# Column halves and quarters of the array in the attention and convolution stage of a two-layer encoder

## The chip, the core and the metric

The kernel runs on one NeuronCore of a Trainium2 chip. The metric is the device time of one launch in microseconds (us). The engines are named as the profile names them: PE is TensorE's matmul, PEld its weight load, DVE is VectorE, ACT is ScalarE, POOL is GpSimd, SP is SyncE, which here only issues DMAs.

## The reference

Two layers, each a half-weighted SwiGLU, a mixing block with attention beside a convolution, a second half-weighted SwiGLU and a norm. There is one sequence of 512 tokens with 1024 features, in float32. What matters here is the mixing block:

```python
def chunk_causal_attention(q, k, v):            # 8 heads, 96 query/key and 64 value features
    for i in range(s // Q_BLOCK):               # query blocks of 128, chunks of 64
        scores = einsum('bhqd,bhkd->bhqk', q[block i], k[: end of block i]) * scale
        scores = where(k_chunk <= q_chunk, scores, -1e30)
        outs.append(einsum('bhqk,bhkd->bqhd', softmax(scores), v))

def conv_group(u_raw, conv_w, conv_b, ln_g, ln_b):
    u = a * sigmoid(g)                          # 512 channels
    y = causal depthwise conv of u, 31 taps; y = y + conv_b
    return silu(layer_norm(y, ln_g, ln_b))

x = x + concatenate([attn, conv]) @ w_out
```

In each block of 128 queries the first 64 must not see the last 64 keys.

## The kernel before

Activations lie with features on the 128 partitions and the 512 tokens along the free axis, so a tile is 128 by 512. Products with big weights are made of three products of operands that are split into a high and a low part (`mm3`, lines 154 to 156). The feed-forward blocks (L373, L374 and most of L154 to L156) take most of the time and are left as they are.

`mix_body` first projects the normed input, then attends, convolves, and projects out. A scheduler of the framework puts the instructions of each engine in order; the order of the source is its priority, and `tc.issue_after` holds a step back until another has been issued. The attention is written as stages of one head each, with lags between them (`ORDER`): `turn` transposes queries and keys (L811, L816, copied by ACT L813 and DVE L818), `scores` makes one product of each block of 128 queries with the keys up to the block's end (L834), adds -1e30 to 64 rows by a small bf16 product (L835), takes the row maximum (DVE L836) and the exponential (ACT L840); `turn_p` transposes the probabilities (L855, copied at L858 by DVE, ACT, DVE); `values` multiplies them with the values (L868), the probabilities as 128 weight columns and the 64 value columns of the head as the moving operand, ten products for a head, and divides by the sums (DVE L875); `turn_out` transposes the result of two heads (L886) and splits it (L161, L162). The attention's operands are plain float32.

The convolution's 512 channels are four groups of 128. `CONV = "DAAD"` says how each is made: groups 0 and 3 on DVE, one instruction for a tap (L922), accumulating in PSUM; groups 1 and 2 with the tap's product on ACT (L926, tile `pr`) and its sum on POOL (L930, tile `y`). Of group 2 thus 30 taps go through ACT and POOL. Then POOL adds the four groups (L944 to L946), PE makes the mean (L948), and while DVE, ACT and POOL finish the LayerNorm, `early_groups` lets PE make the attention's half of three output tiles (`WOG = 3`; `E1`, `E2`, `E3` say at which points). PSUM has seven banks `ps` and one `cv`. Weights come by DMAs that SP issues in order (L136); the low parts of four tiles of `w_out` come by accumulating DMAs from POOL (L142).

Of the kernel before, what the change touches and what calls it, by code (L numbers as in the profile page):

```python
# [7 lines left out]
FP = mybir.dt.float32  # L8
# [3 lines left out]
AF = mybir.ActivationFunctionType  # L12
# [47 lines left out]
JOINED = ("b21", "t3", "t4")  # L60

VECS = [("g1", 8), ("gm", 8), ("g2", 8), ("gp", 8), ("gql", 3), ("gkl", 2),
        ("cw", 4 * CK), ("cb", 4), ("lg", 4), ("lb", 4), ("gq", 1), ("gk", 1)]
VOFF = {}
_o = 0
for _n, _w in VECS:
# [1 line left out]
    _o += _w  # L68
VN = _o
CCOS, CSIN, CID = 0, 64, 128  # L70
CN = 256


@with_exitstack
def encoder_kernel(ctx: ExitStack, tc: tile.TileContext, xT, consts, vecs, rgain, wgu1, wd1, wdq1,
# [11 lines left out]
    def nm(s):  # L87
        uid[0] += 1
        return f"{s}{uid[0]}"
# [7 lines left out]
    def bank():  # L97
        return psum.tile([P, S], FP, tag="ps", name=nm("ps"))
# [517 lines left out]

    def mix_body(kpool, l, gx, norm, done):
        u, order = [], {}

        def kept(dt=FP):  # L620
            return kpool.tile([P, S], dt, tag="m", name=nm("m"), bufs=2 * WIDE)
        ys = [None if kind == "D" else kpool.tile([P, S], FP, tag="y", name=nm("y"), bufs=2) for kind in CONV]

        def glu(pa, pg):
            tg = tmp()
            V.tensor_tensor(tg, pg, R, ALU.mult)
            sg = tmp()
            order["gate"] = A.activation(sg, tg, AF.Sigmoid).ins
            ta = tmp()
            V.tensor_tensor(ta, pa, R, ALU.mult)  # L630
            uc = kept()
            (G if GLUP else V).tensor_tensor(uc, ta, sg, ALU.mult)
# [188 lines left out]
        def scores(h):  # L821
            qT, kT = heads[h]["qk"]
            b01, b2, b3 = bank(), bank(), bank()
            if h % 2 == 0:
                heads[h]["sums"] = small.tile([P, NT, 2], FP, tag="sums", name=nm("sums"), bufs=3)
            sums = heads[h - h % 2]["sums"]
            mx = small.tile([P, NT], FP, tag="mx", name=nm("mx"), bufs=3)
            pi = []
            ps = [slot() for _ in range(3)]
            ps = [ps[0][:, 0:128], ps[0][:, 128:384], ps[1][:, 0:384], ps[2]]  # L830
            for i in range(NT):
                n = (i + 1) * P
                o = (b01[:, 0:128], b01[:, 128:384], b2[:, 0:384], b3)[i]
                T.matmul(o, qT[0:DQ, i * P:(i + 1) * P], kT[0:DQ, 0:n], start=True, stop=False)  # L834
                heads[h]["s"] = T.matmul(o[:, n - 64:n], mrow, mneg, start=False, stop=True).ins  # L835
# [4 lines left out]
                A.activation(p, o, AF.Exp, bias=mx[:, i:i + 1], scale=scqs[i][:, h:h + 1] if QFOLD else 1.0,  # L840
                             accum_out=sums[:, i, h % 2:h % 2 + 1])
                pi.append(p)
            heads[h]["p"] = pi
# [17 lines left out]
        def values(h):  # L861

            if h % 2 == 0:
                heads[h]["po"] = bank()
            po = heads[h - h % 2]["po"].rearrange("p (t h d) -> p t h d", t=NT, h=2)
            for t in range(NT):
                for j in range(t + 1):
                    T.matmul(po[:, t, h % 2], heads[h]["pt"][j][:, (t - j) * P:(t - j + 1) * P],  # L868
                             vs[j][:, h * DV:(h + 1) * DV], start=j == 0, stop=j == t)
            if h % 2 == 0:  # L870
# [4 lines left out]
            V.tensor_tensor(o.rearrange("p (t h d) -> p t h d", t=NT, h=2), po,  # L875
                            rs[:, :, :, None].to_broadcast([P, NT, 2, DV]), ALU.mult)
            heads[h]["o"] = o

        def turn_out(h):

            if h % 2 == 0:
                return
            o = heads[h]["o"]
            ps = bank()
            for t in range(NT):
                T.transpose(ps[:, t * P:(t + 1) * P], o[:, t * P:(t + 1) * P], ident)  # L886
# [27 lines left out]
        for c in range(4):  # L914
            kind = CONV[c]
            acc = psum.tile([P, S], FP, tag="cv", name=nm("cv"), bufs=1) if kind == "D" else ys[c]
            tap = lambda k: cw[:, c * CK + k:c * CK + k + 1]
            A.activation(acc, u[c], AF.Identity, scale=tap(CK - 1), bias=cb[:, c:c + 1])  # L918
            for k in range(CK - 2, -1, -1):
                s = CK - 1 - k  # L920
                if kind == "D":
                    V.scalar_tensor_tensor(acc[:, s:], u[c][:, :S - s], tap(k), acc[:, s:], ALU.mult, ALU.add)  # L922
                    continue
                pr = kpool.tile([P, S], FP, tag="pr", name=nm("pr"), bufs=3)
                if kind == "A":
                    A.activation(pr[:, s:], u[c][:, :S - s], AF.Copy, scale=tap(k))  # L926
                else:
                    G.tensor_scalar(pr[:, s:], u[c][:, :S - s], tap(k), None, ALU.mult)
                with tc.issue_after(order["keys"]) if s >= PAUSE or c > 1 else nullcontext():
                    order["conv"] = G.tensor_tensor(acc[:, s:], acc[:, s:], pr[:, s:], ALU.add).ins  # L930
            if kind == "D":
                A.copy(u[c], acc)
                ys[c] = u[c]
        early = []

        def early_groups(ms):
# [6 lines left out]
        ysum = tmp()  # L943
        G.tensor_tensor(ysum, ys[0], ys[1], ALU.add)  # L944
        G.tensor_tensor(ysum, ysum, ys[2], ALU.add)
        (G if YP else V).tensor_tensor(ysum, ysum, ys[3], ALU.add)  # L946
        pm = bank()
        T.matmul(pm, onesm, ysum, start=True, stop=True)  # L948
        if PRELOAD:
# [291 lines left out]
```

## Time and profile before

| | |
|---|---|
| median of 3 runs | 1800.13 us (1799.9 to 1801.16) |
| the profiled execution | 1798.87 us, span 1797.1 us, granted clock 1.0 |
| PE busy | 1781.8 us, 99% of the span |
| DVE, ACT, POOL busy | 1494.5, 1107.5, 421.5 us |

The span is from the first to the last instruction. The mixing block stands in it twice, with its attention from about 450 to 508 us in layer 0 and from about 1339 to 1398 us in layer 1. A matmul's recorded duration contains its way through the array; what a stream of them costs is read from start to start. A float32 product has two rows in the trace where the program has one.

### The profile page before, as it was taken

The page shows a single profiled execution, that of the slowest core. Times are in us where ns is not written, and L with a number is a line of the kernel's source. Part 1 is how long each engine was busy: PE and PEld are TensorE (multiplying, and loading weights), DVE is VectorE, ACT ScalarE, POOL GpSimd, SP SyncE. Part 2 cuts the span into 40 slices and gives each one's busy share as a digit, 9 for nine tenths or more (in the row PEclk, how much of TensorE's full clock was granted, in tenths as well). Part 3 has the DMA queues.
Part 4 walks back from the last instruction along what each step waited for, and adds up shares of the span by engine and source line. Part 5 has one row for each costly group of instructions (what it writes and reads, how often), then busy time and mean ns, then how long its engine had stood idle before and what let it go on. Part 6 is the DMA issues. An engine that isn't in the chain of part 4 may idle for free.

```text
span 1797.1 us, 29235 instructions
## 1 busy us (share of the span) xinstructions
PE 1781.8 (99%) x11334; PEld 1602.4 (89%) x11334; DVE 1494.5 (83%) x2299; ACT 1107.5 (62%) x1721; POOL 421.5 (23%) x343
## 2 busy tenths in 40 slices
PE   9999999999999999999999999999999999999998
PEld 7899999888788899999888999998978788999997
DVE  7898988589956989898779989876998668989883
ACT  5575756457953575756645757554779435756564
POOL 1000000258943000000310000002689410000002
PEclk9999999999999999999999999999999999999999
DMA  5657575325103466665426575743250125575742
GB/s 168 171 131 182 135 177 123 109 88 134 33 22 102 123 164 161 155 160 132 123 65 170 122 194 122 193 112 111 81 147 7 46 82 160 140 183 134 182 117 74
DMA packets 70413, 226.16 MB, mean 126 GB/s; under 512 B 7937, under 2 KB 8321, under 8 KB 70273
## 3 DMA queue, kind: packets, MB, share of 16 engines
q1 hardware_dynamic: 54000, 169.74, 30.3%
q0 software_dynamic: 16128, 54.53, 18.0%
q8 instruction: 89, 1.46, 0.3%
q14 instruction: 52, 0.42, 0.1%
q10 hardware_dynamic: 144, 0.00, 0.0%
HBM read 222.15 MB, written 2.10 MB: 125 GB/s over the span
## 4 chain that ended last, share of the span: by engine, by line
PE 91%; ACT 3%; DVE 2%; POOL 2%; issue 1%; DMA 0%; SPq 0%; ACTq 0%; POOLq 0%; DVEq 0%
PE ps L154 24%; PE ps L156 23%; PE ps L155 23%; PE ps L373 11%; PE ps L374 6%; PE ps L868 1%; PE ps L834 1%; POOL y L930 1%; ACT pr L926 1%; ACT r L840 1%; PE ps L855 1%; PE ps L198 0%; POOL sck L173 0%; PE ps L217 0%; DVE wl L246 0%
## 5 line engine op out<-in xcount | busy, mean ns | idle before, releaser
L155 PE MATMUL ps<-r,wh 128*128 128x256 f32 (+1 forms) x2540 | 806.8, 318 | 0.0
L154 PE MATMUL ps<-r,wh 128*128 128x256 f32 (+1 forms) x2540 | 803.6, 320 | 2.2 <-ACT wh L138 0.7
L156 PE MATMUL ps<-r,wl 128*128 128x256 f32 (+1 forms) x2348 | 749.2, 321 | 0.0
L154 PEld LDWEIGHTS ps<-r,wh 128*128 128x128 f32 x2540 | 480.5, 189 | 47.0 <-ACT wh L138 3.6
L155 PEld LDWEIGHTS ps<-r,wh 128*128 128x128 f32 x2540 | 481.6, 190 | 35.8 <-DVE r L162 1.5
L156 PEld LDWEIGHTS ps<-r,wl 128*128 128x128 f32 x2348 | 445.1, 190 | 33.5 <-DVE wl L144 0.4
L373 PE MATMUL ps<-xj,wh 128*128 128x512 f32 x864 | 303.9, 392 | 0.0
L138 ACT CAST wh<-raw 128x1024 fp32r<-128x1024 f32 (+3 forms) x148 | 131.9, 899 | 208.1 <-PE ps L155 125.8
L390 POOL DMA_DIRECT2D ls<-in_wgu x72 | 62.7, 871 | 734.7 <-ACT ls L389 595.3
L244 ACT CAST wh<-fr 128x1024 fp32r<-128x1024 f32 (+1 forms) x160 | 157.6, 985 | 104.4 <-DVE fr L410 53.2
L144 DVE TENSOR_TENSOR wl<-raw,wh 128x1024 fp32r<-128x1024 f32 (+3 forms) x132 | 145.3, 1108 | 91.3 <-ACT wh L138 90.9
L246 DVE TENSOR_TENSOR wl<-fr,wh 128x1024 fp32r<-128x1024 f32 (+1 forms) x160 | 182.3, 1139 | 20.3 <-ACT wh L244 20.3
L373 PEld LDWEIGHTS ps<-xj,wh 128*128 128x128 f32 x864 | 161.4, 188 | 30.1
L930 POOL TENSOR_TENSOR y<-y,pr 128x511 f32<-128x511 f32 (+14 forms) x120 | 158.6, 1322 | 54.5 <-ACT pr L926 47.1
L374 PE MATMUL ps<-xj,ls 128*128 128x256 f32 x576 | 161.3, 280 | 0.0
L244 ACT CAST wh<-raw 128x1024 fp32r<-128x1024 f32 (+1 forms) x100 | 98.2, 982 | 45.1 <-PE ps L155 24.2
L246 DVE TENSOR_TENSOR wl<-raw,wh 128x1024 fp32r<-128x1024 f32 (+1 forms) x100 | 113.5, 1135 | 14.2 <-ACT wh L244 13.7
L191 POOL TENSOR_TENSOR r<-r,t 128x512 f32<-128x512 f32 x45 | 75.0, 1676 | 175.6 <-ACT t L187 174.8
L374 PEld LDWEIGHTS ps<-xj,ls 128*128 128x128 f32 x576 | 108.3, 188 | 0.0
L389 ACT ACTIVATE ls<-fr 128x1024 fp32r<-128x1024 f32 (+1 forms) x56 | 56.1, 1002 | 74.5 <-PE ps L374 42.8
L926 ACT ACTIVATE pr<-m,vec 128x511 f32<-128x511 f32 (+14 forms) x120 | 85.7, 736 | 13.2 <-POOL y L930 13.2
L922 DVE SCALAR_TENSOR_TENSOR cv<-m,vec,cv 128x511 f32<-128x511 f32 (+14 forms) x120 | 87.8, 732 | 3.6 <-ACT cv L918 2.2
(241 smaller groups left out, 2944.9 us busy)
## 6 DMA issues: line engine op xcount, KB each, us to landing
fr<-in_wgu SPq DMA_DIRECT2D x112, 512.0 KB, 4.2
ls<-in_wgu POOLq DMA_DIRECT2D x72, 512.0 KB, 6.2
raw<-in_wgu SPq DMA_DIRECT2D x62, 512.0 KB, 4.5
fr<-in_wdq SPq DMA_DIRECT2D x48, 384.0 KB, 4.6
ls<-in_wdq POOLq DMA_DIRECT2D x32, 384.0 KB, 4.8
raw<-in_wd SPq DMA_DIRECT2D x32, 384.0 KB, 3.2
raw<-in_wd SPq DMA_DIRECT2D x32, 256.0 KB, 2.8
raw<-in_wcv SPq DMA_DIRECT2D x16, 512.0 KB, 3.6
```

The source lines that it names most:

```text
L138: order["cast"] = A.copy(hi[:, :w], raw[:, :w]).ins
L144: (G if kind in POOLW.split() else V).tensor_tensor(lo[:, :w], raw[:, :w], hi[:, :w].bitcast(FP), ALU.subtract)
L154: T.matmul(o, lh, rh, start=first, stop=False, skip_group_check=free)
L155: T.matmul(o, lh, rl, start=False, stop=False, skip_group_check=free)
L156: order["mm"] = T.matmul(o, ll, rh, start=False, stop=last, skip_group_check=free).ins
L244: A.copy(hi[:, :w], src[:, :w])
L246: order["lo"] = V.tensor_tensor(lo[:, :w], src[:, :w], hi[:, :w].bitcast(FP), ALU.subtract).ins
L373: T.matmul(o, w[0][:, c], both, start=start and k == 0, stop=False, skip_group_check=True)
L374: last = T.matmul(o[:, 0:HS], w[1][:, c], both[:, 0:HS], start=False, stop=k == 3, skip_group_check=True).ins
L922: V.scalar_tensor_tensor(acc[:, s:], u[c][:, :S - s], tap(k), acc[:, s:], ALU.mult, ALU.add)
L926: A.activation(pr[:, s:], u[c][:, :S - s], AF.Copy, scale=tap(k))
L930: order["conv"] = G.tensor_tensor(acc[:, s:], acc[:, s:], pr[:, s:], ALU.add).ins
```

## The change

Four things are changed in `mix_body`, in both layers.

- **Values.** The two heads of a pair are made together, at the odd head. The 64 value columns of a head are the weights and the probabilities move; one head's result goes to PSUM partitions 0 to 63, the other's to 64 to 127. The result has features on the partitions, so `turn_out`'s four transposes go. The reciprocal sums lie along the partitions and are spread by eight products with the identity (L898), copied by ACT (L901), and multiplied in by DVE (L907).
- **Scores.** Each block's product becomes two of 64 queries, on the two halves of the array's columns: the first without the last 64 keys, the second with all. The mask's product writes the 64 rows and columns that are left out.
- **Convolution.** Of group 2, taps 0 to 15 (by distance) become 16 products on PE (`conv_pe`, L664, issued at head step 3), with 32 weight columns each. POOL builds the diagonal weights (`diag`), DVE zeroes four columns of each of four tiles, and 16 DMAs from SP copy 32 channels each into them, shifted by 0 to 3 tokens. ACT adds the bias on the way out (L666). Taps 16 to 30 stay on ACT and POOL, with four buffers `pr` in place of three.
- **Tail.** The last of the three sums of groups moves from POOL to DVE; `E1 = 1` and `WOG = 4`: four output tiles are begun early, the first ahead of the mean's product.

The program now tells PE a tile of 128 by 64 or 128 by 32 for these products; before, each product had the whole array of 128 by 128.

```diff
-CONV = "DAAD"
+TAPS = (0, 31, 31, 0)
+Q = 32
+PT = 16
+PC = 2
+PSTEP = 3
-E1 = 0
-YP = 1
+E1 = 1
-WOG = 3
+WOG = 4
...
+        diag = kpool.tile([P, PT, Q], FP, tag="m", name=nm("m"), bufs=11)
+        G.tensor_tensor(diag, cst[:, None, CI32:CI32 + Q].to_broadcast([P, PT, Q]),
+                        vv(l, "cp")[:, :, None].to_broadcast([P, PT, Q]), ALU.mult)
...
             glu(*pp)
+            if c != PC:
+                return
+            for i in range(4):
+                v = slot()
+                V.memset(v[:, 0:4], 0.0)
+                for r in range(4):
+                    nc.sync.dma_start(out=v[r * Q:(r + 1) * Q, r:], in_=u[c][i * Q:(i + 1) * Q, 0:S - r])
+                shifted.append(v)
+
+        def conv_pe():
+            ps = bank()
+            for a in range(PT // 4):
+                for i in range(4):
+                    T.matmul(ps[i * Q:(i + 1) * Q, 4 * a:], diag[:, 4 * a + i], shifted[i][:, 0:S - 4 * a],
+                             start=a == 0, stop=a == PT // 4 - 1)
+            A.activation(ys[PC], ps, AF.Identity, bias=vv(l, "cb")[:, PC:PC + 1])
...
-                T.matmul(o, qT[0:DQ, i * P:(i + 1) * P], kT[0:DQ, 0:n], start=True, stop=False)
-                heads[h]["s"] = T.matmul(o[:, n - 64:n], mrow, mneg, start=False, stop=True).ins
+                for r, w in ((0, n - 64), (64, n)):
+                    T.matmul(o[r:r + 64, 0:w], qT[0:DQ, i * P + r:i * P + r + 64], kT[0:DQ, 0:w], start=True, stop=r > 0,
+                             skip_group_check=True)
+                heads[h]["s"] = T.matmul(o[0:64, n - 64:n], mrow[:, 0:64], mneg, start=False, stop=True,
+                                         skip_group_check=True).ins
...
-            for t in range(NT):
-                for j in range(t + 1):
-                    T.matmul(po[:, t, h % 2], heads[h]["pt"][j][:, (t - j) * P:(t - j + 1) * P],
-                             vs[j][:, h * DV:(h + 1) * DV], start=j == 0, stop=j == t)
...
+            pr = bank()
+            for t in range(NT):
+                for i in range(2):
+                    T.matmul(pr[i * DV:(i + 1) * DV, t * P:(t + 1) * P], rs[:, t, i:i + 1].to_broadcast([P, DV]),
+                             ident, start=True, stop=True)
+            r = tmp()
+            A.copy(r, pr)
+            po = bank()
+            for j in range(NT):
+                for i in range(2):
+                    T.matmul(po[i * DV:(i + 1) * DV, j * P:], vs[j][:, (h - 1 + i) * DV:(h + i) * DV],
+                             heads[h - 1 + i]["pt"][j], start=j == 0, stop=j == NT - 1)
             o = tmp()
-            V.tensor_tensor(o.rearrange("p (t h d) -> p t h d", t=NT, h=2), po,
-                            rs[:, :, :, None].to_broadcast([P, NT, 2, DV]), ALU.mult)
+            V.tensor_tensor(o, po, r, ALU.mult)
...
-            o = heads[h]["o"]
-            ps = bank()
-            for t in range(NT):
-                T.transpose(ps[:, t * P:(t + 1) * P], o[:, t * P:(t + 1) * P], ident)
-            at.append(split(ps, kept if len(at) < 2 else slot))
+            at.append(split(heads[h]["o"], kept if len(at) < 1 else slot))
...
+            if step == PSTEP:
+                conv_pe()
...
-        (G if YP else V).tensor_tensor(ysum, ysum, ys[3], ALU.add)
+        V.tensor_tensor(ysum, ysum, ys[3], ALU.add)
```

The first place is PE, at the scores of head 1 in layer 0; before the change, the first two blocks: `ps` is a PSUM bank, the two `r` are keys and queries, and the size is that of the product's output.

```order
L834 MATMUL ps_4815<-r_4737,r_4730 128x128
L835 LDWEIGHTS mrow
L835 MATMUL ps_4815<-mneg,mrow 128x64
L834 MATMUL ps_4816<-r_4737,r_4730 128x384
L835 LDWEIGHTS mrow
L835 MATMUL ps_4816<-mneg,mrow 128x64
```

This is the same place now, and what follows the same head's last block a little later: the convolution's products, `m` being the diagonal weights and the four `r` the shifted tiles.

```order
L860 MATMUL ps_4845<-r_4763,r_4756 64x64
L860 MATMUL ps_4845<-r_4763,r_4756 64x128
L862 LDWEIGHTS mrow
L862 MATMUL ps_4845<-mneg,mrow 64x64
...
L862 MATMUL ps_4847<-mneg,mrow 64x64
L664 MATMUL ps_4872<-r_4635,m_3846 32x512
L664 MATMUL ps_4872<-r_4641,m_3846 32x512
L664 MATMUL ps_4872<-r_4647,m_3846 32x512
L664 MATMUL ps_4872<-r_4653,m_3846 32x512
L664 MATMUL ps_4872<-r_4635,m_3846 32x508
```

Each block has two products of 64 rows in place of one of 128, and sixteen products of 32 rows stand between the scores of head 1 and those of head 2.

The second place is PE's values of the first pair in layer 0; before, one of its two heads (`m` are the values, `r` the turned probabilities):

```order
L868 MATMUL ps_4951<-m_4748,r_4877 128x64 x2
L868 MATMUL ps_4951<-m_4757,r_4884 128x64
L868 MATMUL ps_4951<-m_4748,r_4877 128x64
L868 MATMUL ps_4951<-m_4757,r_4884 128x64
L868 MATMUL ps_4951<-m_4766,r_4891 128x64
L868 MATMUL ps_4951<-m_4748,r_4877 128x64
L868 MATMUL ps_4951<-m_4757,r_4884 128x64
L868 MATMUL ps_4951<-m_4766,r_4891 128x64
L868 MATMUL ps_4951<-m_4775,r_4884 128x64
```

Now, both heads, with the spread sums (`rs`) ahead of them:

```order
L898 MATMUL ps_5074<-cst,rs_5072 64x128 x8
...
L905 MATMUL ps_5085<-r_4933,m_4774 64x512
L905 MATMUL ps_5085<-r_4993,m_4774 64x512
L905 MATMUL ps_5085<-r_4940,m_4783 64x384
L905 MATMUL ps_5085<-r_5000,m_4783 64x384
L905 MATMUL ps_5085<-r_4947,m_4792 64x256
L905 MATMUL ps_5085<-r_5007,m_4792 64x256
L905 MATMUL ps_5085<-r_4940,m_4801 64x128
L905 MATMUL ps_5085<-r_5000,m_4801 64x128
```

Twenty products of a pair with 64 moving columns have become eight with 128 to 512, which alternate between the two halves, and eight with 128.

The third place is the end of layer 0's attention on PE; before, the last pair's transposes, the mean's product (L948) and the first early group:

```order
L868 MATMUL ps_5294<-m_4775,r_5283 128x64
L886 MATMUL ps_5328<-cst,t_5326 128x128 x4
L948 MATMUL ps_5617<-t_5613,onesm 128x512
L154 MATMUL ps_5621<-m_5105,wh_5339 128x512
L155 MATMUL ps_5621<-m_5106,wh_5339 128x512
```

Now, the last two products with the values, the second half of the first early group (bank `ps_5619`; its first half stands a few rows earlier, between the values) and the mean's product, L982:

```order
L905 MATMUL ps_5374<-r_5303,m_4801 64x128
L905 MATMUL ps_5374<-r_5346,m_4801 64x128
L158 MATMUL ps_5619<-r_5357,wh_5391 128x512
L159 MATMUL ps_5619<-r_5358,wh_5391 128x512
L160 MATMUL ps_5619<-r_5357,wl_5393 128x512
L158 MATMUL ps_5619<-r_5385,wh_5391 128x512
L159 MATMUL ps_5619<-r_5386,wh_5391 128x512
L160 MATMUL ps_5619<-r_5385,wl_5393 128x512
L982 MATMUL ps_5636<-t_5632,onesm 128x512
```

The transposes are gone, and an early group stands between the last values and the mean. Line numbers after the change are some 4 to 40 higher than those of the same step before.

More of the change, by code (lines that the diff above doesn't have):

```diff
@@ L913, in mix_body @@
         cw, cb = vv(l, "cw"), vv(l, "cb")
-        for c in range(4):
-            kind = CONV[c]
-            acc = psum.tile([P, S], FP, tag="cv", name=nm("cv"), bufs=1) if kind == "D" else ys[c]
+        for c, n in enumerate(TAPS):
             tap = lambda k: cw[:, c * CK + k:c * CK + k + 1]
[L918 to L921, printed above, removed]
-                    V.scalar_tensor_tensor(acc[:, s:], u[c][:, :S - s], tap(k), acc[:, s:], ALU.mult, ALU.add)
[L923 to L928, printed above, removed]
+            acc = psum.tile([P, S], FP, tag="cv", name=nm("cv"), bufs=1) if n < CK else None
+            if n and c != PC:
+                A.activation(ys[c], u[c], AF.Identity, scale=tap(CK - 1), bias=cb[:, c:c + 1])
+            for s in range(n, CK):
+                k = CK - 1 - s
+                if s == 0:
+                    A.activation(acc, u[c], AF.Identity, scale=tap(k), bias=cb[:, c:c + 1])
+                elif s == n:
+                    A.activation(acc[:, s:], u[c][:, :S - s], AF.Copy, scale=tap(k))
+                else:
+                    V.scalar_tensor_tensor(acc[:, s:], u[c][:, :S - s], tap(k), acc[:, s:], ALU.mult, ALU.add)
+            for s in range(PT if c == PC else 1, n):
+                k = CK - 1 - s
+                pr = kpool.tile([P, S], FP, tag="pr", name=nm("pr"), bufs=4)
+                A.activation(pr[:, s:], u[c][:, :S - s], AF.Copy, scale=tap(k))
@@ L929, in mix_body @@
                 with tc.issue_after(order["keys"]) if s >= PAUSE or c > 1 else nullcontext():
-                    order["conv"] = G.tensor_tensor(acc[:, s:], acc[:, s:], pr[:, s:], ALU.add).ins
-            if kind == "D":
+                    order["conv"] = G.tensor_tensor(ys[c][:, s:], ys[c][:, s:], pr[:, s:], ALU.add).ins
+            if not n:
                 A.copy(u[c], acc)
                 ys[c] = u[c]
+            elif n < CK:
+                V.tensor_tensor(ys[c][:, n:], ys[c][:, n:], acc[:, n:], ALU.add)
@@ L1205 @@
     put("cw", a["conv_w"].reshape(L, CK, 4, P).transpose(3, 0, 2, 1).reshape(P, L, 4 * CK))
+    cp = a["conv_w"][:, ::-1][:, :PT, PC * P:(PC + 1) * P].reshape(L, PT // 4, 4, 4, Q)
+    put("cp", cp.transpose(2, 4, 0, 1, 3).reshape(P, L, PT))
     for name, key in (("gq", "q_norm"), ("gk", "k_norm")):
@@ L1219 @@
     consts[:, CID:CID + P] = np.eye(P, dtype=f32)
+    consts[:, CI32:CI32 + Q] = np.tile(np.eye(Q, dtype=f32), (4, 1))
     arrays = {
```

13 lines of the change are left out of this document (6 added, 7 removed).

## The prediction

> **What bounds the kernel now.** I read the busy shares and the chain of work of the page first.
>
> ```profile
> PE 1781.8 (99%) x11334; PEld 1602.4 (89%) x11334; DVE 1494.5 (83%) x2299; ACT 1107.5 (62%) x1721; POOL 421.5 (23%) x343
> ...
> PE 91%; ACT 3%; DVE 2%; POOL 2%; issue 1%; DMA 0%; SPq 0%; ACTq 0%; POOLq 0%; DVEq 0%
> ```
>
> PE is the bound, and 9% of the chain lies elsewhere. The change touches only the mixing block, so I cut layer 0's attention into stretches: its first heads, its middle, its end, and the LayerNorm behind it.
>
> ```profile
> 449.70:465.00 15.30, 13.46 (x77) 8.60 (x75) 15.30 (x31) 15.30 (x38) 14.02 (x13) 1.00 0.41 87
> 465.00:485.00 20.00, 19.93 (x152) 16.98 (x152) 19.40 (x38) 19.96 (x51) 18.00 (x15) 1.00 0.00 1
> 485.00:508.00 23.00, 22.22 (x178) 19.68 (x176) 15.86 (x32) 15.92 (x37) 20.38 (x17) 1.00 0.01 2
> ```
>
> After the length stand PE, PEld, DVE, ACT and POOL. All four engines are nearly full. In the first stretch PE misses 1.84 us while DVE and ACT have no gap; in the second PE has none; in the third 0.78. The waits of PE say for whom, first in layer 0 (449.7 to 508), then in layer 1 (1339 to 1398):
>
> ```profile
> PE ps L834 <- ACT r L840: 1.5, 3, 0.7
> PE ps L886 <- DVE t L875: 0.8, 1, 0.8
> PE ps L811 <- ACT r L840: 0.3, 1, 0.3
> ...
> PE ps L834 <- ACT r L840: 1.2, 3, 0.4
> PE ps L886 <- DVE t L875: 0.8, 1, 0.8
> PE ps L948 <- POOL t L946: 0.4, 1, 0.4
> PE ps L811 <- ACT r L840: 0.2, 1, 0.2
> ```
>
> So 1.8 and 1.4 us are waits for ACT's exponentials, 0.8 each for the last pair's division, and 0.4 for POOL's sum of the convolution groups. POOL's timeline at the end of layer 0 shows how near it is there, too:
>
> ```profile
> 471.15 31.48 POOL L930 TENSOR_TENSOR y<-y,pr 128x505 f32<-128x505 f32 x24 [0.39 <-ACT pr L926]
> 502.59 1.27 POOL L944 TENSOR_TENSOR t<-m,y 128x512 f32<-128x512 f32 x1
> 503.94 1.27 POOL L945 TENSOR_TENSOR t<-t,y 128x512 f32<-128x512 f32 x1
> 505.29 1.27 POOL L946 TENSOR_TENSOR t<-t,m 128x512 f32<-128x512 f32 x1
> ```
>
> POOL ends at 506.56, and PE's mean (L948) starts at 507.40. PE alone could gain about a microsecond before POOL holds it; the two must come down together, which this change does. What PE's steps cost is read from start to start in its timeline:
>
> ```profile
> 489.97 0.65 PE L834 MATMUL ps<-r,r 96*128 96x256 f32 x2
> 490.45 0.20 PE L835 MATMUL ps<-mneg,mrow 128*128 128x64 bf16 x1
> 490.49 0.46 PE L834 MATMUL ps<-r,r 96*128 96x128 f32 x2
> 490.79 0.19 PE L835 MATMUL ps<-mneg,mrow 128*128 128x64 bf16 x1
> 490.82 0.89 PE L834 MATMUL ps<-r,r 96*128 96x384 f32 x2
> 491.55 0.19 PE L835 MATMUL ps<-mneg,mrow 128*128 128x64 bf16 x1
> 491.58 1.10 PE L834 MATMUL ps<-r,r 96*128 96x512 f32 x2
> 492.52 0.20 PE L835 MATMUL ps<-mneg,mrow 128*128 128x64 bf16 x1
> 492.55 1.28 PE L855 MATMUL ps<-cst,r 128*128 128x128 f32 x10
> 493.67 2.34 PE L868 MATMUL ps<-m,r 128*128 128x64 f32 x20
> 495.85 0.65 PE L834 MATMUL ps<-r,r 96*128 96x256 f32 x2
> ...
> 503.34 0.60 PE L886 MATMUL ps<-cst,t 128*128 128x128 f32 x4
> 503.78 2.34 PE L868 MATMUL ps<-m,r 128*128 128x64 f32 x20
> ```
>
> A float32 product costs 0.30 us with 128 moving columns, 0.48 with 256, 0.73 with 384, 0.94 with 512, always as two passes (x2); some 0.07 of each is fixed. A mask costs 0.03 to 0.04. The ten value products of a head cost 2.18, so 0.109 for each of 20 passes with only 64 moving columns: that is the price of loading 128 weight columns, not of moving. A pair's four transposes cost 0.44.
>
> **The open price: do column halves run side by side?** Every product of before uses the whole array, so no row shows two of them at once. One end is one after another, each at its length's price; the other is side by side, the longer alone. I take side by side: the masks, which start 0.03 us after the product ahead, show that PE starts instructions much faster than it streams them, and two halves share neither weight columns nor PSUM partitions. But the two passes of one product use the same columns and start in order, so of four quarters I expect two to three at work, not four. The Trainium skill, "TensorE: Matmul & The Clock Gate", section "Measured speedup vs the span model", gives 2.38 times for three column tiles; no run here shows it yet, and nothing below uses it.
>
> **Values (PE).** Before, a pair takes 2 x 2.18 + 0.44 = 4.80 us. After, both heads stream 512, 384, 256 and 128 columns: 0.94 + 0.73 + 0.48 + 0.30 = 2.45 for a half, and the second half trails by about a short pass, 0.15: 2.6. The eight spreads of 128 columns cost 8 x 0.30 = 2.4 one after another; side by side 1.1, a little under half. Together 3.7, so -1.1 for each of 8 pairs: **-8.8 us**. One after another it is 4.9 + 2.4 = 7.3, +2.5 a pair, +20.
>
> **Scores (PE).** Before, four products and four masks: 2.45 + 0.13 = 2.58 a head. Side by side the longer half alone remains, 2.45, and part of the fixed 0.07 and of the masks hides under the neighbour: -0.2 for each of 16 heads, **-3.2** (between 0 and -0.4, the mean of both halves). One after another the halves of 64, 192, 320 and 448 columns, at prices between the rows' about 0.18 + 0.39 + 0.61 + 0.83 = 2.0, come on top: +2.0 a head, +32.
>
> **Convolution (PE).** Sixteen products of 500 to 512 columns a layer, 0.93 each: 14.9 one after another, 7.4 two at a time, 3.7 four at a time; I take 5.2, and 10.4 for two layers. They stand in the first stretch, where PE waits 1.8 and 1.4 us for ACT; these 3.2 us it fills. **+7.2** net (between +4.2 and +26.6).
>
> **The other engines.** Fifteen taps of group 2 leave ACT and POOL in each layer.
>
> ```profile
> L926 ACT ACTIVATE pr<-m,vec 128x488 f32<-128x488 f32 (+29 forms) x37 | 26.6, 736 | 1.0 <-POOL y L930 1.0
> ...
> L930 POOL TENSOR_TENSOR y<-y,pr 128x490 f32<-128x490 f32 (+29 forms) x39 | 48.6, 1245 | 5.3 <-ACT pr L926 2.6
> ...
> L858 ACT COPY r<-ps 128x512 f32<-128x512 f32 x16 | 9.9, 617 | 1.0 <-PE ps L855 1.0
> ```
>
> ACT loses 15 x 0.74 = 11 us and gains four copies of the spread sums of 0.62: 8.6 less a layer, though mostly after the first stretch, so its exponentials there come no earlier. POOL loses 15 x 1.245 and the last sum, 20 us, and builds the diagonals early (a sum of 512 columns took 1.27). At the end POOL's 20 us are slack. DVE keeps its work and takes one sum more (0.7 us); in the three stretches it is busy 50.6 of 58.3 us, so the attention cannot shrink by more than about 7 us a layer. That is the floor of the gain, 14 us in all.
>
> **The tail.** The waits of 0.8 for the division and 0.4 for POOL go: the first early group stands ahead of the mean and covers both. Both layers: **-2.0**. What is late next is the LayerNorm, for which PE now has one early group more.
>
> **SP.** The 16 shifted copies stand behind the first four loads of `w_out` and ahead of the other four.
>
> ```profile
> 430.66 23.15 SPq L136 DMA_DIRECT2D raw<-in_wout  x5
> ...
> 437.38 0.69 DVE L632 TENSOR_TENSOR m<-t,t 128x512 f32<-128x512 f32 x1
> ...
> raw<-in_wout SPq DMA_DIRECT2D x7, 512.0 KB, 4.5
> ```
>
> Group 2's input is ready at 438.1 (its last DVE step), and PE wants the copies at about 457, after the scores of head 1. They are 64 KB each; with two turns of the 4.5 us that a 512 KB load takes to land, they are there at 447 to 450. I cost them at nothing; the cover is the 7 us until 457. Queued behind them is `w_out`'s fifth load, which before was issued at 453.8. Behind a late convolution on ACT stand exponentials, and on POOL group 2's sums, with 20 us of slack.
>
> **Switches.** In PE's order 60 places change between 128, 64 and 32 columns. If the array must run empty at each, that costs at most a matmul's way through it:
>
> ```profile
> L855 PE MATMUL ps<-cst,r 128*128 128x128 f32 x160 | 20.7, 274 | 0.0
> ```
>
> 274 ns last one transpose, 112 is from start to start (1.12 for ten), so 0.16 at most, 9.8 us in all. From L834 to L835 and L855 the kind of product changes within 0.03 us with no such gap, though not the tile. I take a tenth: **+1.0**.
>
> Sum: -8.8 - 3.2 + 7.2 - 2.0 + 1.0 = **-5.8 us**. The profiled execution took 1798.87, 1.77 more than its span, which gives 1793.1; it was 1.26 under the median of 1800.13, on whose scale the forecast is 1794.3, rounded **1794**. A difference of 0.2% (3.6 us) is about what the runs can tell.
>
> **Rivals.**
> - *Halves one after another.* Two passes a product, started in order, may not overlap at all. Then values +20, scores +32, convolution +26.6, tail -2: +77, about 1877 on the median's scale. It decides from the point where the halves overlap by less than half. For it: no row shows overlap. Against it: masks start within 0.03 us. Chance 0.10.
> - *The switches drain in full.* +9.8 in place of +1.0: +3.0, 1803, level to slower. For it: every head's scores go to 64 columns and back. Against it: the 0.03 above. The Trainium skill, "TensorEngine Tiling (Array Packing)", section "Key Properties", states that changing the tiling mode drains TensorE; no run here shows a price. Chance 0.12.
> - *Copies or the convolution come late.* PE stands at L664, with scores behind it, and ACT with exponentials; 4 us in each layer give +2, 1802. For it: in the first stretch the DMAs are still at a share of 0.41 with `w_out` (the row's last but one number). Against it: the 7 us of cover. Chance 0.08.
> - *Better than forecast.* Four quarters at work and nothing drained: convolution +4.2, switches 0, -9.8; if the halves also lose the fixed 0.07 of each product, down to DVE's floor, -14: 1786 to 1790. Chance 0.12.
>
> **How the numbers follow.** The forecast has 0.58, with a range of its own of 1788 to 1799; four fifths of it lie under 1796.5 (0.46), most of the rest within 0.2%. Faster: 0.46 + 0.12 and a little of the late copies, 0.60. Same: 0.10 of the forecast and a third of the two middle rivals, 0.16. Slower: halves in turn 0.10, the rest of the middle rivals 0.12 and a little: 0.24. The range runs from DVE's floor and a few us of unknown tail, 1784, to full drains with late copies, 1808; outside is mainly the first rival.
>
> **What would show it.** Right: L905's eight products take about 2.6 us from the first start to the end, L860's four pairs about 2.4, L664's sixteen 4 to 7; POOL's last sum of group 2 ends well before the last values; PE has no wait for POOL ahead of the mean. Wrong: L905 near 4.9 and L664 near 15 (halves in turn); gaps of 0.1 to 0.16 us on PE wherever L860 follows L836 (drains); a wait of L664 for a DMA (late copies); DVE without a gap to the end (its floor).

## The result: slower by 7 us

The changed kernel took 1806.28 us (median of 7 runs, 1803.85 to 1807.88). The kernel before took 1799.04 in the same runs (1797.95 to 1801.16). The ratio is 1.0039, with a 95% interval of 1.0030 to 1.0049: 5 to 9 us slower, where the forecast was 1794.0. The profiled execution took 1807.3 us, 1.8 more than its span.

The page's busy shares and chain of work hardly move:

```profile
span 1805.5 us, 29455 instructions
PE 1786.9 (99%) x11430; PEld 1585.0 (88%) x11430; DVE 1497.1 (83%) x2309; ACT 1094.3 (61%) x1699; POOL 381.4 (21%) x313
...
PE 90%; DVE 4%; ACT 3%; POOL 1%; issue 1%; DMA 0%; SPq 0%; ACTq 0%; DVEq 0%; POOLq 0%
```

PE looks busier by 5.1 us (1786.9 against 1781.8), although the prediction's terms for PE's work (-8.8, -3.2, +10.4 and +1.0) hardly change it. The one new thing is DVE, from 2% to 4% of the chain. So the loss has to be found by stage. Four places of PE's timeline can be matched in every kernel: the first turn of the attention, the mean of the convolution's LayerNorm (L948 before, L982 after), the sums of its variance (L198, L202) and the spreading of the result over the partitions (L217, L221), called the mean, the sums and the spread below. The last three are, before:

```profile
507.40 1.02 PE L948 MATMUL ps<-t,onesm 128*128 128x512 f32 x2
513.84 0.95 PE L198 MATMUL ps<-ones,r 128*128 128x1 f32 x8
517.52 1.02 PE L217 MATMUL ps<-t,ones 128*128 128x512 f32 x2
```

And PE's timeline of the changed kernel, from the last pair of heads on:

```profile
501.39 1.02 PE L905 MATMUL ps<-r,m 128*64 128x512 f32 x2
502.34 0.50 PE L158 MATMUL ps<-m,wh 128*128 128x512 f32 x1
...
503.93 2.37 PE L905 MATMUL ps<-r,m 128*64 128x512 f32 x14
506.23 0.50 PE L158 MATMUL ps<-r,wh 128*128 128x512 f32 x1
...
507.80 0.49 PE L158 MATMUL ps<-r,wh 128*128 128x512 f32 x1 [0.61 <-ACT r L165]
508.53 0.50 PE L159 MATMUL ps<-r,wh 128*128 128x512 f32 x1 [0.23 <-DVE r L166]
508.87 0.40 PE L160 MATMUL ps<-r,wl 128*128 128x512 f32 x1
509.22 1.10 PE L982 MATMUL ps<-t,onesm 128*128 128x512 f32 x2
...
512.70 0.39 PE L160 MATMUL ps<-r,wl 128*128 128x512 f32 x1
515.18 1.84 PE L202 MATMUL ps<-ones,r 128*128 128x1 f32 x8 [2.10 <-DVE r L195]
...
522.02 1.02 PE L221 MATMUL ps<-t,ones 128*128 128x512 f32 x2
```

The first early group (L158 to L160, 12 products) now stands ahead of the mean. Half of it has slipped between the products of the last pair. The other half waits 0.61 and 0.23 us for that pair's split into a high and a low part (ACT L165, DVE L166). Behind the mean only one group is left, 2.9 us, and then PE stands still for 2.10 us until DVE has the sums ready. From L202 to L221 it needs 6.84 us, where before it needed 3.68 for the same work. The windows say why. After each stretch's length stand PE, PEld, DVE, ACT and POOL; the granted clock is the third number from the end. First the attention's three stretches as in the prediction, then the tail:

```profile
449.70:465.00 15.30, 15.18 (x123) 8.60 (x122) 14.61 (x26) 15.30 (x36) 13.80 (x12) 1.00 0.68 180
465.00:485.00 20.00, 19.50 (x166) 13.28 (x165) 19.93 (x41) 18.97 (x49) 16.17 (x14) 1.00 0.00 1
485.00:508.00 23.00, 22.39 (x181) 14.92 (x177) 16.04 (x33) 11.36 (x31) 2.56 (x2) 1.00 0.00 1
...
513.00:515.20 2.20, 0.10 (x2) 0.05 (x1) 1.82 (x3) 0.56 (x1) 0.00 (x0) 0.96 0.00 0
515.20:518.00 2.80, 2.80 (x11) 2.61 (x12) 0.16 (x1) 0.00 (x0) 0.70 (x1) 0.50 0.00 0
518.00:520.00 2.00, 2.00 (x6) 1.53 (x5) 0.69 (x1) 0.00 (x0) 0.33 (x1) 0.50 0.00 0
520.00:521.70 1.70, 1.70 (x5) 1.32 (x4) 0.00 (x0) 0.00 (x0) 0.00 (x0) 0.50 0.04 10
```

After the pause the clock is 0.50 for 6.8 us (515.04 to 521.87), so about 3.4 us are lost while PE is shown as fully busy. That is where the extra busy time of the page comes from. Before, the same place read:

```profile
508.00:521.00 13.00, 13.00 (x59) 10.14 (x58) 7.88 (x14) 5.58 (x10) 1.03 (x1) 1.00 0.00 0
```

The first stretch went as forecast: PE misses 0.12 us there, where it had missed 1.84, and POOL is idle in most of the third. In the second PE misses 0.50 us, where it had missed 0.07.

From these places come the times that the rest of the text uses, in us, for the first and the second layer. E1 is the number of early groups ahead of the mean. The rows below the first two are the experiments of the next section.

| kernel | first turn to mean | mean to spread | both |
|---|---|---|---|
| before (E1=0) | 64.95, 65.24 | 10.12, 10.21 | 75.07, 75.45 |
| after (E1=1) | 66.53, 66.53 | 12.80, 12.68 | 79.33, 79.21 |
| e0_pool | 60.94, 60.96 | 10.74, 10.73 | 71.68, 71.69 |
| e0_dve | 63.95, 64.08 | 10.14, 11.72 | 74.09, 75.80 |
| e1_pool | 66.41, 66.41 | 11.20, 9.62 | 77.61, 76.03 |
| fill | 66.53, 66.67 | 9.69, 9.68 | 76.22, 76.35 |
| before_e1 | 67.95, 67.49 | 11.20, 9.64 | 79.15, 77.13 |
| whole_scores | 62.00, 62.03 | 10.71, 10.74 | 72.71, 72.77 |
| whole_values | 68.19, 68.18 | 10.04, 10.06 | 78.23, 78.24 |
| pool_conv | 65.12, 65.17 | 12.37, 11.80 | 77.49, 76.97 |

The changed kernel minus before is 4.26 and 3.76 us, 8.0 of the 8.4 by which the spans differ.

### The profile page after: what moved, and what is told of

It is laid out like the page before. It is cut to its first block, busy times and chain, and to the rows that moved or that the text cites. A ratio compares the mean times of both kernels' runs of the same rounds, so it can differ in the third digit from the quotient of the medians.

```text
span 1805.5 us, 29455 instructions
## 1 busy us (share of the span) xinstructions
PE 1786.9 (99%) x11430; PEld 1585.0 (88%) x11430; DVE 1497.1 (83%) x2309; ACT 1094.3 (61%) x1699; POOL 381.4 (21%) x313
## 4 chain that ended last, share of the span: by engine, by line
PE 90%; DVE 4%; ACT 3%; POOL 1%; issue 1%; DMA 0%; SPq 0%; ACTq 0%; DVEq 0%; POOLq 0%
PE ps L158 23%; PE ps L160 23%; PE ps L159 23%; PE ps L377 11%; PE ps L378 6%; ACT pr L960 1%; PE ps L905 1%; ACT r L868 1%; PE ps L860 1%; PE ps L883 1%; PE ps L202 1%; POOL sck L177 1%; PE ps L898 0%; PE ps L221 0%; DVE kn L810 0%
## 5 line engine op out<-in xcount | busy, mean ns | idle before, releaser
L158 PE MATMUL ps<-r,wh 128*128 128x256 f32 (+1 forms) x2556 | 811.6, 321 | 3.5 <-ACT r L165 1.5
L160 PE MATMUL ps<-r,wl 128*128 128x256 f32 (+1 forms) x2364 | 757.0, 322 | 0.0
L158 PEld LDWEIGHTS ps<-r,wh 128*128 128x128 f32 x2556 | 484.4, 190 | 50.1 <-ACT wh L142 3.4
L160 PEld LDWEIGHTS ps<-r,wl 128*128 128x128 f32 x2364 | 449.0, 190 | 34.8 <-DVE wl L148 0.7
L962 POOL TENSOR_TENSOR y<-y,pr 128x495 f32<-128x495 f32 (+29 forms) x90 | 120.7, 1342 | 46.6 <-ACT pr L960 41.0
L484 DVE SCALAR_TENSOR_TENSOR x<-ps,x 128x512 f32<-128x512 f32 x112 | 76.8, 686 | 8.0 <-PE ps L160 7.4
```

What stands on the lines that cost most here:

```text
L158: T.matmul(o, lh, rh, start=first, stop=False, skip_group_check=free)
L160: order["mm"] = T.matmul(o, ll, rh, start=False, stop=last, skip_group_check=free).ins
L484: return V.scalar_tensor_tensor(v, o.rearrange("p (m t) -> p m t", m=2), 0.5 * sign, v, ALU.mult, ALU.add).ins
L962: order["conv"] = G.tensor_tensor(ys[c][:, s:], ys[c][:, s:], pr[:, s:], ALU.add).ins
```

## Experiments

**Theory:** the tiles gain about what was forecast, and the two edits at the tail (one early group ahead of the mean, the last sum on DVE) lose more than that, by waits and by the clock. **Rival:** the tiles themselves lose (switches, the convolution on PE, halves in turn), and the tail merely shows it. The first four runs vary the tail, the next the tail of the old kernel, the last three one part of the change each.

**e0_pool: the tiles kept, both edits of the tail undone.**

```diff
-E1 = 1
+E1 = 0
...
-        V.tensor_tensor(ysum, ysum, ys[3], ALU.add)
+        G.tensor_tensor(ysum, ysum, ys[3], ALU.add)
```

> The changed kernel with no early group ahead of the mean's product (E1 = 0) and the last sum of the convolution groups back on POOL. Theory (the tail took the gain: the mean waits behind an early group and a DVE sum, then only one group covers the LayerNorm's sums, PE idles 2.1 us, and the granted clock is halved for 6.5 us): the mean starts right after the last values, two groups cover the sums, no wait at the sums, clock 1.0, and the 3.3 us a layer by which the attention is shorter show: 1792 to 1795. Rival (the smaller tiles themselves cost the time, by switches and by a lower clock): 1803 to 1807.

Measured: 1792.34 (1791.21 to 1792.92), ratio to before 0.9961 [0.9948, 0.9973]. It is the fastest kernel of this study, 13.9 us under the changed one. In PE's timeline the mean follows the last value product at once, and two groups leave a wait of 0.35; in POOL's the last sum was done at 501.09, before PE could use it:

```profile
501.60 2.32 PE L905 MATMUL ps<-r,m 128*64 128x512 f32 x16
503.85 1.12 PE L982 MATMUL ps<-t,onesm 128*128 128x512 f32 x2
...
510.84 1.02 PE L202 MATMUL ps<-ones,r 128*128 128x1 f32 x8 [0.35 <-DVE r L195]
...
514.59 1.02 PE L221 MATMUL ps<-t,ones 128*128 128x512 f32 x2
```

```profile
499.81 1.28 POOL L980 TENSOR_TENSOR t<-t,m 128x512 f32<-128x512 f32 x1
```

So the tiles gain, and the two edits of the tail together are at fault: the theory's 1792 to 1795 holds, and the rival falls. Outside the places of the table e0_pool is 1.1 us slower than before (the spans differ by 6.0, the table by 7.15). It keeps `WOG = 4`, which also groups the output tiles otherwise; that number was not varied alone.

**e0_dve: only the early group put back behind the mean.**

```diff
-E1 = 1
+E1 = 0
```

> Only E1 = 0; the last sum stays on DVE, where it stands behind the split of the last pair. Theory: the mean cannot start before that sum, at about 1.8 us after the last values, and PE stands empty for these (nothing is queued ahead of the mean); the sums are then covered by two groups. An idle stretch of 2 us is there as before, only earlier, so the clock may fall once more: 1796 to 1806, above the variant with both. Rival (the order of the early group alone is at fault): 1792 to 1795.

Measured: 1798.52 (1797.42 to 1802.24), ratio 0.9999 [0.9989, 1.0008]: no difference from before, inside the forecast range. Here DVE's sum alone costs 6.2 us. POOL had its part at 498.70, but on DVE the sum is queued behind the split of the last pair, which waits for ACT; DVE's timeline, and the mean on PE:

```profile
503.00 0.69 DVE L908 TENSOR_TENSOR t<-ps,t 128x512 f32<-128x512 f32 x1 [1.65 <-PE ps L905]
504.38 0.69 DVE L166 TENSOR_TENSOR r<-t,r 128x512 fp32r<-128x512 f32 x1 [0.68 <-ACT r L165]
504.99 0.69 DVE L980 TENSOR_TENSOR t<-t,m 128x512 f32<-128x512 f32 x1
```

```profile
505.82 1.10 PE L982 MATMUL ps<-t,onesm 128*128 128x512 f32 x2 [2.93 <-DVE t L980]
```

**e1_pool: only the sum put back on POOL.**

```diff
-        V.tensor_tensor(ysum, ysum, ys[3], ALU.add)
+        G.tensor_tensor(ysum, ysum, ys[3], ALU.add)
```

> Only the last sum back on POOL; the early group stays ahead of the mean. Theory: the mean still stands behind the early group and its wait for the last pair's split, so it starts at most 0.5 us earlier, one group covers the sums, PE idles about 2 us there and the clock is halved as before: 1803 to 1807. Rival (the sum's place on DVE is what delays the mean): 1794 to 1797.

Measured: 1805.84 (1800.77 to 1807.79), ratio 1.0030 [1.0018, 1.0042], like the changed kernel and as forecast. With the group ahead of the mean the sum on DVE costs nearly nothing more, since the group waits for the same split that the sum is queued behind: the mean starts 0.23 us after the group's last L160 (508.36 to 508.59), where the changed kernel has 0.35. The two edits overlap, and with the group in place the sum hardly matters. The six runs also move in step with the clock, with one program: their mean granted clocks were 1.000, 0.999, 0.996, 0.996, 0.995 and 0.995, and their times, in that order, 1800.77, 1802.54, 1805.31, 1806.38, 1806.61 and 1807.79. One program spreads over 7 us, the slower the lower its clock.

**fill: the changed kernel, with four spare products of 288 columns on PE where it idled, ahead of the sums.**

```diff
-        r = st.token(CW)
+        with tc.issue_after(order["product"]) if "product" in order else nullcontext():
+            spare = bank()
+            for _ in range(4):
+                order["spare"] = T.matmul(spare[:, 0:CN], ident, cst, start=True, stop=True).ins
+        with tc.issue_after(order["spare"]):
+            r = st.token(CW)
```

> The changed kernel with four spare products of 288 columns (about 2.1 us, their result is not used) on PE in the gap ahead of the sums. Theory (idle PE lowers the clock): the sums start as late as before, but the clock stays 1.0 and the 12 products behind them cost 0.23 us each in place of 0.43: 3 us less a layer, 1799 to 1801. Rival (the clock falls for another reason, such as the small tiles ahead): the half clock stays, 1806 to 1807.

Measured: 1800.67 (1800.26 to 1801.07), ratio 1.0007 [0.9998, 1.0015], as the theory had it. Work that nobody needs takes 5.6 us off the changed kernel. The spare products end as the sums come, the clock stays up, and the spread of the 11 runs is 0.8 us:

```profile
512.17 2.10 PE L993 MATMUL ps<-cst 128*128 128x288 f32 x8
514.43 1.02 PE L202 MATMUL ps<-ones,r 128*128 128x1 f32 x8 [0.15 <-DVE r L195]
```

```profile
513.00:521.00 8.00, 7.85 (x37) 5.92 (x36) 3.81 (x7) 0.99 (x2) 1.03 (x1) 1.00 0.01 2
```

The sums come no earlier (mean to L202 5.96 in both), so the 5.6 us are the clock's. The other 8.3 us down to e0_pool are the order's own.

**before_e1: the kernel before, with only E1 changed.**

```diff
-E1 = 0
+E1 = 1
```

> The kernel before with one number changed, E1=1: one early group of the output projection moves from behind the mean to ahead of it. Theory (the loss of the change lies in this order, not in the tiles): the group stands between the last values and the mean and waits there for the last pair's division; behind the mean two groups cover the LayerNorm in place of three, PE idles 1 to 2 us ahead of the sums' product, and the clock may fall as it did in the kernel after. 1.5 to 4 us a layer: 1802 to 1807, against 1799.4 for before. Rival (the loss comes from the tiles: copies of sums on ACT, one more sum on DVE, 32-row tiles): without these the order alone costs nothing, 1798 to 1800.

Measured: 1804.59 (1803.62 to 1806.02), ratio 1.0032 [1.0020, 1.0043]. One number moves the old kernel by 5.4 us, without a tile or a sum changed. In the first layer, first PE's waits, then the clock:

```profile
PE ps L198 <- DVE r L191: 2.1, 1, 2.1
...
PE ps L886 <- DVE t L875: 0.8, 1, 0.8
```

```profile
517.50:521.00 3.50, 3.50 (x10) 2.69 (x9) 0.69 (x1) 0.00 (x0) 0.69 (x1) 0.51 0.00 0
456.00:459.50 3.50, 3.50 (x15) 2.78 (x14) 3.21 (x7) 3.50 (x11) 3.27 (x4) 0.51 0.93 210
```

One clause of the theory fails: the group neither covers the division's wait nor waits there itself. The last pair's transposes wait 0.8 as before, and the group starts behind them (506.69 and 507.10). And the sums, with one group ahead of them, wait 2.1. The clock fell twice in the first layer of the profiled execution, the second time behind that wait. The order alone thus costs in the old kernel too, by the uncovered wait and the clock; the rival is refuted.

**whole_scores: e0_pool with the scores undivided.**

```diff
-                for r, w in ((0, n - 64), (64, n)):
-                    T.matmul(o[r:r + 64, 0:w], qT[0:DQ, i * P + r:i * P + r + 64], kT[0:DQ, 0:w], start=True, stop=r > 0,
-                             skip_group_check=True)
-                heads[h]["s"] = T.matmul(o[0:64, n - 64:n], mrow[:, 0:64], mneg, start=False, stop=True,
-                                         skip_group_check=True).ins
+                T.matmul(o, qT[0:DQ, i * P:(i + 1) * P], kT[0:DQ, 0:n], start=True, stop=False)
+                heads[h]["s"] = T.matmul(o[:, n - 64:n], mrow, mneg, start=False, stop=True).ins
```

> e0_pool with the scores as one product of 128 queries again and masks over 128 columns; values and convolution stay on column tiles. The trace of after gives the split scores and their masks 1.56 us less of PE a layer, and the transposes behind them and the switches 2 to 4 us more. Theory (the switches eat what the split saves): within 2 us of e0_pool, 1790.5 to 1794.5. Rival of the prediction's sum (3.2 us saved in two layers, switches 1.0 in all): 2 to 3.5 us slower than e0_pool, 1794.5 to 1796.

Measured: 1794.10 (1793.53 to 1795.84), ratio 0.9971 [0.9960, 0.9982]. The ratios' intervals overlap with e0_pool's, but every run is slower than every run of e0_pool; the medians differ by 1.8. The traces, with 1.06 and 1.07 us a layer from first turn to mean, say that the split saves about 2 us in all. That is inside the theory's range, near its upper end: the switches eat most of what the split saves.

**whole_values: e0_pool with the values, the division and the transposes as before.**

```diff
-            pr = bank()
...
-            for j in range(NT):
-                for i in range(2):
-                    T.matmul(po[i * DV:(i + 1) * DV, j * P:], vs[j][:, (h - 1 + i) * DV:(h + i) * DV],
-                             heads[h - 1 + i]["pt"][j], start=j == 0, stop=j == NT - 1)
+            for t in range(NT):
+                for j in range(t + 1):
+                    T.matmul(po[:, t, h % 2], heads[h]["pt"][j][:, (t - j) * P:(t - j + 1) * P],
+                             vs[j][:, h * DV:(h + 1) * DV], start=j == 0, stop=j == t)
...
```

> e0_pool with the values as before: ten products a head with 64 moving columns, division on DVE, four transposes a pair. The prediction's sum gives 8.8 us for this part, the traces 5.8 us of PE a layer less what its switches cost. Expected by the sum: 8 to 10 us slower than e0_pool, 1800 to 1802. Rival (other engines or switches took most of it): 1795 to 1799.

Measured: 1804.66 (1804.50 to 1805.57), ratio 1.0030 [1.0018, 1.0042]: 12.3 us slower than e0_pool, more than either expectation. First turn to mean grows by 7.25 and 7.22 us a layer, 0.8 of it the wait for the division that is back; mean to spread gives 0.7 back. The values are the part that carries the change.

**pool_conv: e0_pool with all 31 taps of the third group on ACT and POOL.**

```diff
...
-            if step == PSTEP:
-                conv_pe()
...
-            for s in range(PT if c == PC else 1, n):
+            for s in range(1, n):
```

> e0_pool without the products of the third convolution group: its 31 taps go through ACT and POOL as before, with no diagonals and no shifted copies. PE has 3.5 us a layer less to do and would reach the mean at about 500 in the first layer; POOL ends its sums at 505 to 506.5. Theory (POOL then bounds the mean, the products buy PE's gain its room): the mean stands behind a wait of 4 to 6 us for POOL, and the time is 3 to 7 us above e0_pool, 1795 to 1799, near before. Rival (POOL's sums move up with the start, the products are not needed): 1786 to 1791.

Measured: 1802.95 (1801.54 to 1804.44), ratio 1.0020 [1.0011, 1.0030]: 10.6 us slower than e0_pool, and slower than my range. PE starts the last pair's value products at 500.3 and then waits for POOL:

```profile
PE ps L959 <- POOL t L957: 4.3, 1, 4.3
```

```profile
504.50:511.50 7.00, 4.61 (x9) 3.00 (x10) 3.71 (x6) 2.78 (x5) 2.26 (x2) 0.52 0.00 0
```

The wait was forecast; the clock at half for 6.8 us behind it was not. So the sixteen products on PE repay their 3.5 us a layer: without them PE gains nothing that it can keep, because POOL's sums hold the mean.

## Why the prediction was wrong

**The step that failed is the tail**, put at -2.0 with the words that the first early group covers both waits, and that PE then "has one early group more" for the LayerNorm. WOG does rise from 3 to 4, but the fourth group goes behind the spread; between the mean and the sums stood groups 0 and 1, and now stands group 1 alone. I counted the groups and not their places. From the mean's start to the sums DVE and ACT need 5.96 us in the changed kernel. PE's own work there was 6.44 us before, the mean and two groups, and hid it; the mean and one group are 3.86 us and leave 2.10 open. In the first layer the changed kernel pays, against e0_pool:

- waits for the split inside the group, 0.61 + 0.23 = 0.84;
- the last pair's value products torn in two: 0.95 + 2.30 from start to start against 2.25, so 1.0;
- the group's twelve products, broken up by this and by the waits: 1.59 + 2.99, less the 0.84 and 12 x 0.23, so 1.0;
- the wait for the sums, 2.10 against 0.35: 1.75;
- half clock for 6.8 us: 3.4.

That is 8.0 against 7.65 measured, so the list is complete to within what its terms are good for. By the medians the new tail costs 13.9 us in both layers, where my term had a gain of 2.0. The waits that this term counted (0.8 and 0.8 for the division, 0.4 for POOL) did go, but not by the group: in e0_pool, with no group ahead of the mean, they are gone too. The transposes that waited for the division no longer exist, and POOL is done early; the sums there wait 0.35 a layer instead.

That 1806.28 still lies under the 1808 at which I ended the range is luck. That end stood for full drains with late copies, and the time was lost elsewhere.

**The other terms together came out better than forecast.** e0_pool is the changed kernel without the new tail, and at 1792.34 it lies 7.1 us under before (1799.41 in the same runs). The sum without the tail's term was -3.8, and -5.8 with the waits that are gone there as well. Single terms missed on both sides.

- *Halves side by side: right.* PE's timeline of the changed kernel has a pair's eight value products in 2.2 us, from L905 to the next line, and eight spreads in 0.9:

```profile
488.93 2.40 PE L905 MATMUL ps<-r,m 128*64 128x512 f32 x16
491.11 0.33 PE L860 MATMUL ps<-r,r 96*64 96x64 f32 x3
...
491.82 0.20 PE L862 MATMUL ps<-mneg,mrow 128*64 128x64 bf16 x1
491.86 1.20 PE L860 MATMUL ps<-r,r 96*64 96x448 f32 x4
492.63 0.19 PE L862 MATMUL ps<-mneg,mrow 128*64 128x64 bf16 x1
492.98 1.75 PE L883 MATMUL ps<-cst,r 128*128 128x128 f32 x14
...
496.05 1.09 PE L898 MATMUL ps<-cst,rs 128*64 128x128 f32 x16
496.97 0.60 PE L905 MATMUL ps<-r,m 128*64 128x512 f32 x2
```

- *Values: -8.8 was too little.* The pair takes 2.2 + 0.9 = 3.1, not 3.7: the second half does not trail, and the spreads gain more than half. That is 1.7 a pair and 13.6 in all by this reckoning; whole_values, with the division's wait in it, gives 12.3.
- *Scores: right as a net, from larger parts.* Over the first layer's eight heads L834 took 19.25 us of PE and L860 15.4, start to start, and the masks went from 2.01 to 4.3: from a mask's start to the next product it is 0.20 to 0.35 us where that product uses 128 columns (492.63 to 492.98), and at most 0.04 where it uses 64 (491.82 to 491.86). The split alone was forecast at -3.2, and the switches, most of them its own, at +1.0; whole_scores gives -1.8 for both. Its first layer shows the parts, with the scores whole and split: 19.4 and 15.4 for the scores, 2.0 and 4.3 for the masks, 17.4 and 18.0 for the transposes. So the split gains 4.0 a layer, and its switches take 2.9 of it back.
- *Switches: dearer than +1.0.* The masks' 0.29 a head alone make 2.3 us a layer, and the transposes, which the switches surround, took 2.0 us a layer more than before (the two turns and L883). Together 8.6 us in two layers, near the 9.8 of the rival that had them drain in full; but not all of the 2.0 need be switches, and 1.4 of it stands in whole_scores as well. The Trainium skill, "TensorEngine Tiling (Array Packing)", section "Key Properties", states that a change of the tiling mode drains TensorE; the 0.20 to 0.35 against 0.04 us agrees, and the gains of the halves are net of it.
- *Convolution: cheaper.* L664's 32 passes in four quarters took 3.5 us a layer, not 5.2:

```profile
456.61 3.60 PE L664 MATMUL ps<-r,m 128*32 128x512 f32 x32
460.14 0.65 PE L860 MATMUL ps<-r,r 96*64 96x192 f32 x4
```

  I had expected two to three quarters at work, and it was four (the last section has the rows). The attention's waits for ACT fell from 1.8 us to less than 0.2 in the first layer and from 1.4 to 0.5 in the second, so most of the 3.2 us of cover was there.
- *Copies: at nothing, but by less than I thought.* They made PE wait nowhere. I had them landed at 447 to 450, ahead of 457. In the first layer's trace SP starts the last of the sixteen at 452.4, and the fastest of them take 2.0 us to land, so at most 2.2 us were left until L664.

Of the rivals, halves in turn is refuted by the rows above, and the late convolution by the same. Full drains were nearly right in their price and wrong in the result, since the halves gained more. "Better than forecast" had the four quarters right and the undrained switches wrong; the 1792.3 without the new tail lies in the forecast's own range. The signs that the prediction named for being right came nearly all true, L905 and L664 even shorter than stated, and none of them looks behind the mean, where the time was lost. None of the four rivals had the tail as its place; the rival that ends slower should have been the order of the early groups, and the row to read was PE's own timeline between L948 and L198, which has two groups and no wait.

Not explained: in the first layer PE waits 0.9 us for DVE at the turn of the second key (L841), in all kernels with the new tiles, also in pool_conv (0.8), which has no shifted copies. Before has no such wait in the first layer; in the second it is 0.2 with and without the tiles.

## What to carry to other kernels

Work that only fills time has to stand inside the wait that it is to fill: count what lies between the producer's start and the consumer, place by place, and not how much of it there is. A filler that itself needs the last result of the stage is no filler. When a bound engine comes down in time, what the others must deliver at its end has to come down with it: here the convolution on PE (10.6 us) and the sum on the idle POOL (6.2 us) decide whether the 12 us of the values are kept.

## What the runs showed of the hardware

**A pause of 2.1 us can halve PE's clock, depending on where it lies on a fixed grid.** In the profiled executions the granted clock fell to 0.50 for either 3.41 us (e1_pool 515.54 to 518.95, before_e1 456.09 to 459.50 and 517.53 to 520.94, e0_dve 1395.26 to 1398.68, pool_conv 1399.01 to 1402.42) or 6.83 us (the changed kernel in both layers, from 515.04 and 1409.33; pool_conv in the first, from 504.71). The two falls of before_e1 start 61.44 us apart, 18 times 3.4133. The falls of the two layers start 894.29 us apart both in the changed kernel and in pool_conv, 262 times 3.4133. So in these executions the clock is decided on a grid of 3.4133 us, for the next piece.

The grid also tells some pauses apart. In e0_dve a border of it cuts the first layer's pause of 2.93 us into 1.5 and 1.4, and the clock held; in the second layer 2.5 us of the same pause lie in one piece, and it fell. In e1_pool's second layer 1.84 us of the 2.1 lie in one piece, and the clock held; in the changed kernel's first layer it is 1.96, and it fell. That would explain why the times of e1_pool spread over 7 us, but only one of its six executions has a trace. The share that must be idle stays open: in before_e1 the fall at 517.53 has 1.73 us of pause ahead of it in its piece, and 0.9 us of one-column products (L198); the fall at 456.09 comes after waits of only 1.2 us, and the kernel before, with nearly the same waits at this place, kept its clock.

The Trainium skill, "TensorE: Matmul & The Clock Gate", section "What's actually happening", describes a free-running window of 3.4 us, which these lengths and distances bear out. The Trainium skill, same page, section "Why this matters for your kernels", asks for no idle gaps over about 3 us; here 2.1 us were enough, repeatedly, and the measurement decides.

**Four quarters of the array work at once.** Sixteen float32 products of about 500 columns in four quarters took 3.5 us, 0.22 a product, where one whole-array product of 512 columns took 0.94 before. PEld's timeline shows how: the weight loads come four at a time, one for each quarter.

```profile
457.06 0.13 PEld L664 LDWEIGHTS ps<-r,m 128*32 128x32 f32 x4 [0.30 <-issue]
457.49 0.13 PEld L664 LDWEIGHTS ps<-r,m 128*32 128x32 f32 x4 [0.30 <-issue]
```

Four passes thus take 0.43 us together, close to the 0.47 of one whole-array pass. PEld is idle for 0.30 of each 0.43, so the weight loads are not what sets this pace.
